# Late operand splits, the engines of the last merges, and the buffer of one output weight in a hybrid decoder layer

## The chip, the cores and the metric

The kernel runs on one core of a Trainium2 chip. The metric is the device time of one execution in microseconds (us), smaller is better. Five engines of the core work side by side, each on its own instruction stream in order: TensorE (PE, matrix products), VectorE (DVE), ScalarE (ACT), GpSimd (POOL) and SyncE (SP, which issues most loads). They wait for one another by semaphores.

## What is computed

One inference step of a one-layer decoder for a prompt of 1024 tokens and 8 samples of 4 tokens (1056 rows in all, width 1024): a sliding-window attention branch and a retention branch (4 heads, key width 128, value width 256) on one input projection, merged by sigmoid gates, projected by `w_o`, and a ConvFFN behind it. Cut to what matters here:

```python
def trunk_layer(x, pos, ...):
    xn = rms_norm(x, g_pre_mix)
    h = xn @ w_in
    q_a, k_a, v_a, q_r, k_r, v_r, gate_r, gm_a, gm_r = jnp.split(h, split_points(), axis=-1)
    ...
    o_a = banded_window_attn(q_a, k_a, v_a, pos, sinks)
    ...
    o_r, new_s = retention(qr, kr, vr, ret_s0.astype(jnp.float32))
    o_r = head_rms(o_r).reshape(B, T, V_R).astype(x.dtype)
    y_a = o_a @ w_a_proj
    y_r = (jax.nn.silu(gate_r) * o_r) @ w_r_proj
    mixed = (jax.nn.sigmoid(gm_a) * y_a + jax.nn.sigmoid(gm_r) * y_r) @ w_o
    x = x + rms_norm(mixed, g_post_mix)
    f, new_conv = conv_ffn(rms_norm(x, g_pre_ffn), conv_ctx, w_up, conv_w, conv_b, w_down)
    x = x + rms_norm(f, g_post_ffn)
```

## The kernel before

**Numbers as pairs.** Every matrix operand is held as two float32r tiles, a high part (a cast on ACT) and a low part (source minus high part, on DVE); the function `split` (and `w_split` for the input weights) does both, so a weight's split is one ACT instruction and one DVE instruction (all `L223`, with two inputs in SBUF). A product `mm3` is three matmuls: high x high, high x low, low x high (`L255` to `L257`).

**Seven products for eight.** The large projections (`w_in`, `w_r_proj`, the FFN) are computed two by two blocks by a scheme of Strassen's kind with seven products, A11, A12, A22, S1, S2, S3, S4. Its operands are sums of blocks: on the weight side, `in_split` splits seven weights for each unit of two columns; on the activation side `x_sums(j)` builds the operands `ex` of S2, S3 and A22 for each half j of the rows. A product is 12 matmuls of 128x264.

**The stream.** `stream()` is a Python generator that emits the input projection of the retention branch and of all gates, one product at each `yield`; `adv(n)` takes n products out of it. The other stages place these products between their own steps. 16 units stand in `ORDER`, each with j = 0 and 1. After some products the PSUM banks are evicted into the tile `pair` by a copy on ACT (`L926`) and additions on DVE (`L949` behind S4, `L951` behind S3). The weights' buffers are `wsp` (tags `hi` and `lo`, three buffers each) and, for each seventh split, a tile `w7x` of another pool; `NSPL` counts the splits. The raw weights (`w_raw`, loaded by SP) are freed when their last split is done.

**What stands around the stream's start.** `attn_proj(0..3)` (the attention branch's projection, which also uses `wsp`), `x_sums(0)` and `x_sums(1)`. In the last one, before the operands of S3 and A22, `first_weights` begins the first unit's splits (EARLY, five of them). Then a pool is closed and its memory goes to the pool `rs` with the constants of the rotary embedding and the samples' tiles.

**The samples.** `sample(h)` emits one head of the samples' retention step (five steps, between which `adv(3)` stands): loads, a product with the states `s0`, the state's update, and at the end `finish` (normalisation on ACT and POOL) and `turn`, two transposes on PE (`L1012`), whose result goes to `z8`.

**The prompt's retention** follows (blocks of 128 rows of each head, with `adv` in between), then the projection by `w_r_proj`: `PORD` gives its seven products; `z_weights(n)` loads and splits 14 weights (n = 0 to 13, here z0 to z13). The results go to the eight tiles `Gr[0..7]`, by evictions on ACT and DVE (`L1273` to `L1283`; `L1279` for S3 and S1, `L1283` for S4). As soon as a half of a tile is complete, `merge(m, half)` multiplies it by a gate (`L1267`, input `g_in`) and adds the other branch (`L1268`, input `a_in`): half 0 after A12 (tiles 0 to 3) and A22 (tiles 4 to 7), half 1 after S1 (tiles 4 to 7) and S4 (tiles 0 to 3). `merged_to_X` splits the merged halves into the operand of `w_o` (`xh` on ACT, `xl` on DVE). In between, `weights` loads and splits the eight parts of `w_o`, `wo[0]` to `wo[7]`; the list at its end says from which pool each takes its buffers: `wop`, `tpool` (16 buffers that are also those of the `Gr` tiles) or, for None, `wsp`.

**The output loop** runs over nine tiles of rows (`tt`), each 8 x 2 products of 128x512 in `w_part(hf, k, ...)`; the first tile runs over k in the order `LATE`. Behind it come the norm, and the first products of `w_up`, whose weights take buffers of `wsp`.

What is emitted is put in order for each engine by a scheduler of the framework, except instructions marked by `PIN` or `pinned`, which keep their place.

Of the kernel before, what the change touches and what calls it, by code (L numbers as in the profile page):

```python
# [18 lines left out]
P = 128  # L19
D = 1024  # L20
KD = D // P
# [99 lines left out]
def trunk(ctx, tc, I, O):  # L121
# [200 lines left out]
    NSPL = [0]  # L322
# [471 lines left out]
    begun = []  # L794

    def x_sums(j):

        b12 = b12_X(j)
        t2, t3, t, u1 = tiles = [p2.tile([P, 4, HW], F32, name="ts%d" % q) for q in range(4)]
        combos(j, 0, HW, tiles[:3])  # L800
        t1(j, u1, t2, V)
        split(*b12, u1)
        for p, src in ((S2, t2), (S3, t3), (A22, t)):
            if j and p == S3:
                first_weights()
                PIN[0] = True
            ex1[p, j] = [TT("ex", (P, 4, HW), F32R) for _ in range(2)]
            split(*ex1[p, j], src)
        PIN[0] = False
# [24 lines left out]
    def first_weights():  # L834

        ws = in_split(ORDER[0])
        next(ws)
        next(ws)
        begun.extend((p, next(ws)) for p in EARLY[:5])
        begun.append(ws)  # L840

# [3 lines left out]
    x_sums(1)  # L845

    ph_stack.close()
    rp = pool("rs", 1, stack=ph_stack)
# [52 lines left out]
    def stream():  # L901

        ws = begun.pop()
        ops = dict(begun)
        ops[S3] = next(ws)
# [3 lines left out]
        for i, n in enumerate(ORDER):  # L909
            for j in range(2):  # L910
# [17 lines left out]
                for p in (A11, S1, A22, S2, A12, S4, S3):  # L928
                    if p == A22:
                        if last is not None:  # L930
                            product(A22, *last)
                        if j == 0:
                            ops[A22] = next(ws)
                            ws = coming
                            if i + 1 < len(ORDER):
                                next(ws)
# [15 lines left out]
                    if p == S2:  # L952
                        flush()
                    if j and i + 1 < len(ORDER):
# [19 lines left out]
    def flush():  # L974
        while PEND:
            PEND.pop(0)()

    rcos, rsin = ST("rcos", (P, T)), ST("rsin", (P, T))
# [45 lines left out]
    def sample(h):  # L1024
# [50 lines left out]
        S.copy(out=z8[:, h], in_=turn(pt, finish(os8, NS, 1, h, 1)))  # L1075

    for n in range(2):
        load_s0(n)
    adv(18)
    for h in range(4):  # L1080
        for _ in sample(h):
            adv(3)

# [140 lines left out]
    for g in range(3):  # L1224
        load_v(g)
    coming, behind = ahead(0), None
# [13 lines left out]
    adv(len(ORDER) * 14 - 8 - 78 - 4 * NBLK - 1)  # L1240
# [19 lines left out]
    def merge(m, half):  # L1260
# [5 lines left out]
        eng = G if m < 4 else V  # L1266
# [33 lines left out]
    for pi, p in enumerate(PORD):  # L1300
# [19 lines left out]
        for m in {0: (0,), 1: (1,), 2: (2,), 3: (3, 4), 4: (5,), 5: (6,), 6: (7,)}.get(pi, ()):  # L1320
            wo.append(weights(1, D, [(lambda r: r[:, 0], w_o[m * P:(m + 1) * P, :])],
                              [wop, wop, tpool, tpool, tpool, tpool, tpool, None][m]))
# [12 lines left out]
    LATE = (0, 1, 2, 3, 4, 7, 5, 6)  # L1335
# [416 lines left out]
```

## Time and profile before

| | |
|---|---|
| three runs, median (lowest to highest) | 1674.64 us (1672.92 to 1675.68) |
| the profiled execution | 1673.6 us |
| its span, from the first to the last instruction | 1671.8 us |
| mean granted clock of TensorE | 0.997 of full speed |
| instructions | 32491 |
| HBM read, written | 184.24 MB, 87.49 MB |

The times that follow are microseconds from the start of the span. The samples' stage lies at about 300 to 412, the prompt's retention from there to about 690, the projection by `w_r_proj` and the merges up to 797, the first tile of `w_o` from 797 to 816, the FFN from about 905 to the end. A profile's row of the timeline gives the start, the duration, the engine, the line in the kernel, the operation, the tile written and the tiles read, its size, and in brackets how long the engine was idle before it and what ended that.

### The profile page before, as it was taken

To read this page: it belongs to the slowest core of one execution; us is meant where nothing else is said; L and a number is where in the kernel's file an instruction comes from. 1 tells how busy PE (TensorE), PEld (TensorE's weight loads), DVE (VectorE), ACT (ScalarE), POOL (GpSimd) and SP (SyncE) were. 2 spreads that over 40 slices of the span, in tenths; PEclk is the share of its full clock that TensorE was granted. 3 is DMA by queue.
4 is the path that set the end of the run, shared out by engine and by line. 5 is a ranking of instruction groups with operands and counts; after the bars stand their busy time and mean duration, and the time that the engine had idled before them with its cause. 6 is when DMAs were issued, how large, how long until landed. Compare 5 with 4: busy or idle time off the path is not lost.

```text
span 1671.8 us, 32491 instructions
## 1 busy us (share of the span) xinstructions
PE 1629.8 (97%) x12551; PEld 1587.6 (95%) x12551; DVE 1229.3 (74%) x2035; ACT 860.4 (51%) x1882; POOL 474.1 (28%) x686
## 2 busy tenths in 40 slices
PE   8999999898999999999999999999999999999997
PEld 7999989888999999999688999999999999999997
DVE  7887738799556566478847988888898988455476
ACT  6565634355655655554333655555555556443343
POOL 4242430456343433250412122212322223111111
PEclk9999999999999999999999999999999999999999
DMA  7312232445676775597523144545444548866664
GB/s 199 67 46 72 70 78 99 151 137 170 211 243 217 239 236 178 186 296 213 186 89 103 51 142 159 172 147 172 159 160 160 173 158 257 243 192 195 195 187 144
DMA packets 273291, 273.88 MB, mean 164 GB/s; under 512 B 23040, under 2 KB 234272, under 8 KB 273121
## 3 DMA queue, kind: packets, MB, share of 16 engines
q1 hardware_dynamic: 239377, 155.25, 32.0%
q0 software_dynamic: 33760, 116.57, 20.1%
q8 instruction: 98, 1.61, 0.4%
q14 instruction: 56, 0.46, 0.1%
HBM read 184.24 MB, written 87.49 MB: 163 GB/s over the span
## 4 chain that ended last, share of the span: by engine, by line
PE 68%; DVE 3%; DMA 2%; issue 1%; ACT 1%; SPq 0%; POOL 0%; DVEq 0%; ACTq 0%; POOLq 0%
PE ps_m L257 9%; PE ps_m L256 9%; PE ps_m L255 9%; PE ps_t L256 8%; PE ps_t L255 8%; PE ps_t L257 8%; PE ps_q L255 4%; PE ps_q L257 4%; PE ps_q L256 4%; DVE xl L223 1%; DMA zt<-in_w_r_proj 1%; PE ps_b L1155 1%; PE ps_a L1159 1%; PE ps_b L1157 1%; PE ps_t L461 0%
## 5 line engine op out<-in xcount | busy, mean ns | idle before, releaser
L255 PE MATMUL ps_q<-xh,w 128*128 128x264 f32 x512 | 152.4, 298 | 5.4 <-DVE pair L949 3.0
L223 DVE SCALAR_TENSOR_TENSOR w_lo<-w_raw,w_hi 128x1024 fp32r<-128x1024 f32 x83 | 106.7, 1290 | 65.5 <-ACT w_hi L228 59.9
L255 PE MATMUL ps_t<-xh,w_hi 128*128 128x264 f32 (+2 forms) x524 | 149.0, 284 | 0.0
L256 PE MATMUL ps_t<-xl,w_hi 128*128 128x264 f32 (+2 forms) x524 | 148.9, 284 | 0.0
L257 PE MATMUL ps_t<-xh,w_lo 128*128 128x264 f32 (+2 forms) x524 | 148.2, 283 | 0.0
L257 PE MATMUL ps_m<-xh,w_lo 128*128 128x264 f32 x512 | 145.7, 285 | 0.5 <-DVE w_lo L223 0.5
L255 PE MATMUL ps_m<-xh,w_hi 128*128 128x264 f32 x512 | 146.0, 285 | 0.0
L256 PE MATMUL ps_q<-xl,w 128*128 128x264 f32 x512 | 145.9, 285 | 0.0
L256 PE MATMUL ps_m<-xl,w_hi 128*128 128x264 f32 x512 | 145.5, 284 | 0.0
L257 PE MATMUL ps_q<-xh,w 128*128 128x264 f32 x512 | 145.4, 284 | 0.0
L223 DVE SCALAR_TENSOR_TENSOR w<-w_raw,w 128x512 fp32r<-128x512 f32 x152 | 113.3, 751 | 36.9 <-ACT w L331 35.4
L1500 DVE SCALAR_TENSOR_TENSOR c_out<-u_ext,fconst,c_out 128x1024 f32<-128x1024 f32 x96 | 122.3, 1281 | 2.0 <-ACT c_out L1496 0.5
L228 ACT CAST w_hi<-w_raw 128x1024 fp32r<-128x1024 f32 x62 | 65.2, 1052 | 104.5 <-PE ps_t L256 75.0
L331 ACT CAST w<-w_raw 128x512 fp32r<-128x512 f32 x152 | 93.9, 622 | 37.9 <-DVE w_raw L223 22.9
L255 PEld LDWEIGHTS ps_q<-xh,w 128*128 128x128 f32 x512 | 96.6, 189 | 7.5 <-DVE pair L949 4.4
L257 PEld LDWEIGHTS ps_t<-xh,w_lo 128*128 128x128 f32 x524 | 98.8, 189 | 0.0
L255 PEld LDWEIGHTS ps_t<-xh,w_hi 128*128 128x128 f32 x524 | 98.7, 188 | 0.0
L256 PEld LDWEIGHTS ps_t<-xl,w_hi 128*128 128x128 f32 x524 | 98.7, 188 | 0.0
L257 PEld LDWEIGHTS ps_m<-xh,w_lo 128*128 128x128 f32 x512 | 96.4, 188 | 0.8 <-DVE w_lo L223 0.7
L256 PEld LDWEIGHTS ps_q<-xl,w 128*128 128x128 f32 x512 | 96.6, 189 | 0.5
L256 PEld LDWEIGHTS ps_m<-xl,w_hi 128*128 128x128 f32 x512 | 96.3, 188 | 0.0
L255 PEld LDWEIGHTS ps_m<-xh,w_hi 128*128 128x128 f32 x512 | 96.3, 188 | 0.0
(447 smaller groups left out, 6045.7 us busy)
## 6 DMA issues: line engine op xcount, KB each, us to landing
w_raw<-in_w_up SPq DMA_DIRECT2D x48, 512.0 KB, 4.1
w_raw<-in_w_in SPq DMA_DIRECT2D x42, 512.0 KB, 4.6
w_raw<-s_d SPq DMA_DIRECT2D x60, 256.0 KB, 4.0
t_d<-t POOLq DMA_DIRECT2D x24, 528.0 KB, 3.9
t<-t_d POOLq DMA_DIRECT2D x24, 528.0 KB, 5.1
t<-in_w_down SPq DMA_DIRECT2D x48, 256.0 KB, 4.4
s_d<-t POOLq DMA_DIRECT2D x24, 512.0 KB, 3.5
w_raw<-in_w_down SPq DMA_DIRECT2D x36, 256.0 KB, 5.7
```

The lines of the kernel that those rows point to most:

```text
L223: pinned(V.scalar_tensor_tensor(out=out, in0=in0, scalar=1.0, in1=in1, op0=mult, op1=op))
L228: pinned(S.copy(out=hi, in_=src))
L255: TE.matmul(ps, wh, xh, start=start, stop=False, **kw)
L256: TE.matmul(ps, wh, xl, start=False, stop=False, **kw)
L257: TE.matmul(ps, wl, xh, start=False, stop=stop, **kw)
L331: S.copy(out=t[:, 0:4], in_=src)
L1155: TE.matmul(po, sT, vt, start=True, stop=tt == 0)
L1157: TE.matmul(po, q, state["s"], start=False, stop=True)
L1159: TE.matmul(pk, kt, vt, start=True, stop=True)
L1500: V.scalar_tensor_tensor(out=c[:, NS:], in0=u[:, g, NU + t:NU + t + SEQ], scalar=sc[t], in1=c[:, NS:], op0=mult, op1=add)
```

## The change

Five things change. (1) The last two operands of `x_sums(1)`, those of S3 and A22, are no longer split in `x_sums` but, by the new function `operand`, behind the first four calls of the stream; `first_weights` and `begun` go, and the pool is closed after that. (2) The splits are counted from 2 instead of 0, so the fifth split of each unit (S4), not the seventh (A22) in the first unit, takes the tile `w7x`; the stream takes the weights of S3 and A22 of the first unit later. (3) The transposes at a sample head's end are kept in a list `turns` and emitted behind the first three products after the next head's first step; the counts of `adv` follow. (4) The merges of half 1 swap engines: tiles 4 to 7 on POOL, tiles 0 to 3 on DVE; half 0 stays. (5) `wo[6]` takes its buffers from `wsp` instead of `tpool`, and the first tile of the output loop runs over k in plain order.

```diff
--- before.py
+++ after.py
@@ -319,7 +319,7 @@
         split(hi, lo, raw)
         return hi, lo
 
-    NSPL = [0]
+    NSPL = [2]
     wx = {}
 
     def w_split(src, eng):
@@ -791,7 +791,6 @@
     EARLY = (A11, S1, S2, A12, S4, S3)
     COLS = [(QR0 + P * h, KR0 + P * h) for h in range(4)]
     COLS += [(c, c + P) for b in (GR0, GA0, GM0) for c in range(b, b + D, 2 * P)]
-    begun = []
 
     def x_sums(j):
 
@@ -802,11 +801,13 @@
         split(*b12, u1)
         for p, src in ((S2, t2), (S3, t3), (A22, t)):
             if j and p == S3:
-                first_weights()
-                PIN[0] = True
-            ex1[p, j] = [TT("ex", (P, 4, HW), F32R) for _ in range(2)]
-            split(*ex1[p, j], src)
-        PIN[0] = False
+                return t3, t
+            operand(p, j, src)
+
+    def operand(p, j, src):
+
+        ex1[p, j] = [TT("ex", (P, 4, HW), F32R) for _ in range(2)]
+        split(*ex1[p, j], src)
 
     def in_split(n):
 
@@ -831,21 +832,10 @@
         yield w_split(a21, V)
         yield w_split(a22, V)
 
-    def first_weights():
-
-        ws = in_split(ORDER[0])
-        next(ws)
-        next(ws)
-        begun.extend((p, next(ws)) for p in EARLY[:5])
-        begun.append(ws)
-
     for mm in range(4):
         attn_proj(mm)
     x_sums(0)
-    x_sums(1)
-
-    ph_stack.close()
-    rp = pool("rs", 1, stack=ph_stack)
+    late = x_sums(1)
 
     def ST(name, shape, dt=F32, **kw):
         return rp.tile(list(shape), dt, name=name, **kw)
@@ -900,9 +890,10 @@
 
     def stream():
 
-        ws = begun.pop()
-        ops = dict(begun)
-        ops[S3] = next(ws)
+        ws = in_split(ORDER[0])
+        next(ws)
+        next(ws)
+        ops = {p: next(ws) for p in EARLY[:5]}
         coming = in_split(ORDER[1])
         next(coming)
         last, nh = None, 0
@@ -929,7 +920,7 @@
                     if p == A22:
                         if last is not None:
                             product(A22, *last)
-                        if j == 0:
+                        if j == 0 and i:
                             ops[A22] = next(ws)
                             ws = coming
                             if i + 1 < len(ORDER):
@@ -951,6 +942,12 @@
                         V.tensor_tensor(out=c22, in0=bk[1], in1=c22, op=add)
                     if p == S2:
                         flush()
+                    if p == S4 and S3 not in ops:
+                        ops[S3] = next(ws)
+                    if p == S3 and A22 not in ops:
+                        ops[A22] = next(ws)
+                        ws = coming
+                        next(ws)
                     if j and i + 1 < len(ORDER):
                         nxt[p] = next(ws)
                         if p == S4 and i + 2 < len(ORDER):
@@ -975,6 +972,13 @@
         while PEND:
             PEND.pop(0)()
 
+    adv(4)
+    PIN[0] = True
+    for p, t in zip((S3, A22), late):
+        operand(p, 1, t)
+    PIN[0] = False
+    ph_stack.close()
+    rp = pool("rs", 1, stack=ph_stack)
     rcos, rsin = ST("rcos", (P, T)), ST("rsin", (P, T))
     ld.dma_start(out=rcos, in_=I["rcos"])
     ld.dma_start(out=rsin, in_=I["rsin"])
@@ -1072,14 +1076,20 @@
         os8 = ST("t8", (P, 256))[:NS]
         S.copy(out=os8, in_=po[NS:2 * NS])
         V.tensor_tensor(out=os8, in0=po[0:NS], in1=os8, op=add)
-        S.copy(out=z8[:, h], in_=turn(pt, finish(os8, NS, 1, h, 1)))
-
+        o = finish(os8, NS, 1, h, 1)
+        turns.append(lambda: S.copy(out=z8[:, h], in_=turn(pt, o)))
+
+    turns = []
     for n in range(2):
         load_s0(n)
-    adv(18)
+    adv(14)
     for h in range(4):
         for _ in sample(h):
             adv(3)
+            while turns:
+                turns.pop()()
+    adv(2)
+    turns.pop()()
 
     for nm in "kv":
         pin(st.dma_start(out=O[nm + "_sample"][0].rearrange("b r k d -> b r (k d)")[:, 0:P - DS, :],
@@ -1223,6 +1233,7 @@
         load_qk(g)
     for g in range(3):
         load_v(g)
+    adv(0)
     coming, behind = ahead(0), None
     for g in range(NBLK):
         f, coming = coming, ahead(g + 1)
@@ -1237,7 +1248,7 @@
         behind = (g,) + m
     adv(1)
     tail(*behind)
-    adv(len(ORDER) * 14 - 8 - 78 - 4 * NBLK - 1)
+    adv(len(ORDER) * 14 - 8 - 80 - 4 * NBLK - 1)
     for n in range(4):
         load_z(n, quarters(ST("zt", (P, T), bufs=3)) if n < 2 else TT("z_raw", (P, 4, HW)))
     for _ in STR:
@@ -1263,7 +1274,7 @@
         for t, d in zip(ga, (gm_d[KD + m], a_d[m])):
             ld.dma_start(out=t, in_=halves_of(d)[:, :, half])
         v = halves_of(Gr[m])[:, :, half]
-        eng = G if m < 4 else V
+        eng = V if (m < 4) == half else G
         eng.tensor_tensor(out=v, in0=v, in1=ga[0], op=mult)
         eng.tensor_tensor(out=v, in0=v, in1=ga[1], op=add)
 
@@ -1319,7 +1330,7 @@
             merged_to_X(0)
         for m in {0: (0,), 1: (1,), 2: (2,), 3: (3, 4), 4: (5,), 5: (6,), 6: (7,)}.get(pi, ()):
             wo.append(weights(1, D, [(lambda r: r[:, 0], w_o[m * P:(m + 1) * P, :])],
-                              [wop, wop, tpool, tpool, tpool, tpool, tpool, None][m]))
+                              [wop, wop, tpool, tpool, tpool, tpool, None, None][m]))
     merged_to_X(1)
 
 
@@ -1332,7 +1343,7 @@
     J1B = NS + 7 * P - 3 * HW
     raws = {j: [tr.tile([P, 4, HW], F32, name="t%d" % q) for q in range(3)] for j in range(1)}
 
-    LATE = (0, 1, 2, 3, 4, 7, 5, 6)
+    LATE = range(KD)
     for tt in [0, 4, SMP, 1, 2, 3, 5, 6, 7]:
         r_ = rows(tt)
         xt = TT("xt2", (P, D))[:r_]
```

Three places show how the instructions move. The lines of the new kernel are 9 lower in the stream (`L917` was `L926`, `L934` was `L943`, `L940` was `L949`) and 11 higher from the merges on (`L1278` was `L1267`, `L1290` was `L1279`, `L1294` was `L1283`).

First, ACT at the start of the stream, before. `w7` are high parts of the first unit's weights, `y_a` results of `attn_proj`, `ex` the operands of A22 and S3 for j = 1, `pair` the first eviction:

```order
L331 CAST w7_3590<-w_raw_3539 128x512
L786 COPY y_a_3447<-ps_a_3476 128x288
L331 CAST w7_3557<-w_raw_3537 128x512
L228 CAST ex_3560<-ts1_3519 128x1056
L228 CAST ex_3564<-ts2_3520 128x1056
L926 COPY pair_3595<-ps_q2_3597 128x264
L926 COPY pair_3595<-ps_q1_3598 128x264
L926 COPY pair_3595<-ps_q0_3596 128x264
```

And in the new kernel, up to the same operands:

```order
L786 COPY y_a_3403<-ps_a_3432 128x288
L786 COPY y_a_3447<-ps_a_3448 128x384
L786 COPY y_a_3447<-ps_a_3462 128x384
L917 COPY pair_3562<-ps_q2_3564 128x264
L917 COPY pair_3562<-ps_q1_3565 128x264
L331 CAST w7_3678<-w_raw_3539 128x512
L786 COPY y_a_3447<-ps_a_3476 128x288
L331 CAST w7_3662<-w_raw_3539 128x512
L917 COPY pair_3562<-ps_q0_3563 128x264
L228 CAST ex_3619<-ts1_3519 128x1056
L228 CAST ex_3623<-ts2_3520 128x1056
```

The three evictions stood behind both operands' casts and now stand ahead of them; the fifth weight (`w7x`) has moved further up, ahead of the rows shown.

Second, DVE in the last part of `w_r_proj`, before, up to the low part of z13 (`w_lo_9772`). `Gr4` to `Gr7` are the tiles whose half 1 S1 completes, `xl` the low parts of merged halves:

```order
L1267 TENSOR_TENSOR Gr7_8834<-Gr7_8834,g_in_9568 128x2x264
L1279 TENSOR_TENSOR Gr5_8832<-ps_m_9653,Gr5_8832 128x264
L1279 TENSOR_TENSOR Gr5_8832<-ps_t_9667,Gr5_8832 128x264
L1267 TENSOR_TENSOR Gr4_8831<-Gr4_8831,g_in_9647 128x2x264
L1279 TENSOR_TENSOR Gr6_8833<-ps_m_9694,Gr6_8833 128x264
L223 SCALAR_TENSOR_TENSOR xl_110<-Gr6_8833,xh_109 128x264
L1268 TENSOR_TENSOR Gr7_8834<-Gr7_8834,a_in_9569 128x2x264
L223 SCALAR_TENSOR_TENSOR xl_110<-Gr6_8833,xh_109 128x264
L1267 TENSOR_TENSOR Gr5_8832<-Gr5_8832,g_in_9681 128x2x264
L1279 TENSOR_TENSOR Gr6_8833<-ps_t_9708,Gr6_8833 128x264
L223 SCALAR_TENSOR_TENSOR w_lo_9772<-w_raw_9768,w_hi_9771 128x1024
```

The same place in the new kernel; `w_lo_9765` is the low part of `wo[6]`:

```order
L223 SCALAR_TENSOR_TENSOR w_lo_9765<-w_raw_9762,w_hi_9764 128x1024
L223 SCALAR_TENSOR_TENSOR xl_110<-Gr6_8833,xh_109 128x264
L1290 TENSOR_TENSOR Gr6_8833<-ps_m_9694,Gr6_8833 128x264
L223 SCALAR_TENSOR_TENSOR xl_110<-Gr6_8833,xh_109 128x264
L1279 TENSOR_TENSOR Gr7_8834<-Gr7_8834,a_in_9569 128x2x264
L1290 TENSOR_TENSOR Gr6_8833<-ps_t_9708,Gr6_8833 128x264
L1290 TENSOR_TENSOR Gr7_8834<-ps_m_9728,Gr7_8834 128x264
L1290 TENSOR_TENSOR Gr7_8834<-ps_t_9742,Gr7_8834 128x264
L223 SCALAR_TENSOR_TENSOR xl_110<-Gr4_8831,xh_109 128x264
L223 SCALAR_TENSOR_TENSOR xl_110<-Gr7_8834,xh_109 128x264 x2
L1294 TENSOR_TENSOR Gr0_8827<-ps_m_9619,Gr0_8827 128x264
L223 SCALAR_TENSOR_TENSOR w_lo_9772<-w_raw_9768,w_hi_9771 128x1024
```

Ahead of z13's low part two merges of half 1 have gone, and `wo[6]`'s low part, the two evictions of `Gr7`, the `xl` of `Gr4` and `Gr7` and one eviction of `Gr0` have come.

Third, POOL's merges of half 1 in the new kernel:

```order
L1278 TENSOR_TENSOR Gr4_8831<-Gr4_8831,g_in_9647 128x2x264
L1278 TENSOR_TENSOR Gr5_8832<-Gr5_8832,g_in_9681 128x2x264
L1279 TENSOR_TENSOR Gr4_8831<-Gr4_8831,a_in_9648 128x2x264
L1279 TENSOR_TENSOR Gr5_8832<-Gr5_8832,a_in_9682 128x2x264
L1278 TENSOR_TENSOR Gr6_8833<-Gr6_8833,g_in_9722 128x2x264
L1278 TENSOR_TENSOR Gr7_8834<-Gr7_8834,g_in_9756 128x2x264
L1279 TENSOR_TENSOR Gr6_8833<-Gr6_8833,a_in_9723 128x2x264
L1279 TENSOR_TENSOR Gr7_8834<-Gr7_8834,a_in_9757 128x2x264
```

Before, the eight rows here were those of `Gr0` to `Gr3`, whose half 1 is complete only after S4.

## The prediction

> **What bounds the kernel now.** I read the page's busy shares first, then the table of TensorE's waits, then windows cut by stage, then the timelines of the stages that lose time.
>
> ```profile
> PE 1629.8 (97%) x12551; PEld 1587.6 (95%) x12551; DVE 1229.3 (74%) x2035; ACT 860.4 (51%) x1882; POOL 474.1 (28%) x686
> ```
>
> ```profile
> 283.00:330.00 47.00, 41.31 (x307) 40.23 (x307) 29.20 (x40) 18.44 (x41) 16.01 (x14) 1.00 0.46 144
> 330.00:420.00 90.00, 81.37 (x635) 77.04 (x635) 85.48 (x130) 48.26 (x132) 53.16 (x45) 1.00 0.46 148
> 420.00:690.00 270.00, 269.12 (x2079) 263.47 (x2078) 157.40 (x336) 155.27 (x380) 93.99 (x156) 1.00 0.68 214
> 690.00:777.00 87.00, 85.86 (x702) 85.33 (x701) 61.17 (x76) 47.76 (x73) 27.59 (x26) 1.00 0.83 257
> 777.00:818.00 41.00, 37.01 (x230) 33.18 (x229) 39.82 (x66) 16.59 (x38) 14.32 (x10) 0.96 0.79 234
> 818.00:1590.00 772.00, 772.00 (x6045) 754.47 (x6044) 585.27 (x907) 386.19 (x731) 168.21 (x286) 1.00 0.51 162
> ```
>
> Columns: window, its length, busy PE, PEld, DVE, ACT, POOL, then the granted clock, DMA share and GB/s. PE sets the end: its work is unchanged by the edit, so only idle or slowed PE time can come or go. The edit touches three windows with some: 5.7 us idle in 283:330, 8.6 in 330:420, 4.0 in 777:818 (with a mean clock of 0.96). In 330:420 DVE is busy 85.48 of 90, in 777:818 39.82 of 41: there DVE is the bound and PE follows it.
>
> **Stream start (283 to 330).** Three timelines of before: ACT, PE, DVE (start, length, instruction, and in brackets the idle time before it with what ended it).
>
> ```profile
> 297.19 0.62 ACT L331 CAST w<-w_raw 128x512 fp32r<-128x512 f32 x1 [1.34 <-PE ps_a L256]
> ...
> 298.53 2.04 ACT L228 CAST ex<-ts 128x1056 fp32r<-128x1056 f32 x2
> 300.48 0.94 ACT L926 COPY pair<-ps_q 128x264 f32<-128x264 f32 x3
> ```
>
> ```profile
> 300.91 0.39 PE L255 MATMUL ps_q<-xh,w 128*128 128x264 f32 x1 [2.27 <-ACT pair L926]
> ...
> 317.84 0.39 PE L255 MATMUL ps_q<-xh,w 128*128 128x264 f32 x1 [1.76 <-DVE pair L949]
> ```
>
> ```profile
> 297.85 1.51 DVE L223 SCALAR_TENSOR_TENSOR w<-w_raw,w 128x512 fp32r<-128x512 f32 x2 [10.10 <-ACT w L331]
> ...
> 305.95 0.69 DVE L223 SCALAR_TENSOR_TENSOR s<-w_raw 128x512 f32<-128x512 f32 x1 [1.87 <-DMA w_raw<-in_w_in]
> ...
> 314.03 1.46 DVE L1039 TENSOR_TENSOR v<-vs,v 32x256 fp32r<-32x256 f32 x1
> ...
> 317.36 0.43 DVE L949 TENSOR_TENSOR pair<-ps_q,pair 128x264 f32<-128x264 f32 x1
> ...
> 330.31 0.69 DVE L223 SCALAR_TENSOR_TENSOR s<-w_raw 128x512 f32<-128x512 f32 x1 [1.73 <-DMA w_raw<-in_w_in]
> ```
>
> The fifth weight split waits for `attn_proj`'s last product (ACT, 297.19), the operand casts `ex` stand ahead of the evictions, and PE waits 2.27 us. Changed: the fifth split goes to a buffer nobody holds, and the late operands stand behind the evictions. The first eviction then needs 298.53, not 300.48: about 2 us of the 2.27 go. The next unit's raw weights, freed by that split, come sooner. DVE's row from 305.95 to the second `L949` loses one weight split and `v`'s two subtractions (the second took 1.46): the 1.76 us wait goes too. The two come to about 4 us of PE. What is late next is the DVE-bound stage, which starts from the second unit's raw weights (330.31). These wait on SP behind a raw load that the fourth split of unit 1 frees; I have that some 3.3 us sooner, between 2.0 (the first wait alone) and 4.0 (both). So **A = -3.3 us**. Ends: 0, if DVE's backlog eats it, and -6, if the deferred turn's wait (next) and the smaller ones of 0.6 to 1.0 in the samples also go.
>
> **Sample turns.**
>
> ```profile
> PE ps_b L1012 <- ACT o L1006: 1.3, 1, 1.3
> ```
>
> This is a row of PE's waits (total, times, longest). One turn in four was waited for. With three products in between it is covered. Since DVE, busy 85.48 of 90, sets that stage, PE would only wait elsewhere: 0, at best the -1.3 in A's low end. Products pulled ahead are 14 + 4 for 18, and 2 at the end, so the later stages stand two products on; PE is full there (269.12 of 270): 0.
>
> **Merges and the seventh w_o weight (777 to 818).** First the loss of before, on PE, with DVE's split that ends it.
>
> ```profile
> 806.47 0.39 PE L256 MATMUL ps_m<-w_loT,xh 128*128 128x512 f32 x1
> 806.70 0.40 PE L257 MATMUL ps_m<-w_hiT,xl 128*128 128x512 f32 x1
> 807.23 0.50 PE L255 MATMUL ps_m<-w_hiT,xh 128*128 128x512 f32 x1
> 811.58 0.80 PE L256 MATMUL ps_m<-w_loT,xh 128*128 128x512 f32 x1 [3.85 <-DVE w_loT L223]
> 812.17 0.63 PE L257 MATMUL ps_m<-w_hiT,xl 128*128 128x512 f32 x1
> ...
> 815.02 0.39 PE L255 MATMUL ps_m<-w_hiT,xh 128*128 128x512 f32 x1
> ```
>
> ```profile
> 806.13 1.05 ACT L246 CAST w_hiT<-w_raw 128x1024 fp32r<-128x1024 f32 x1 [2.77 <-DVE xl L223]
> ```
>
> Full pitch of a 128x512 product is 0.23 us (806.47 to 806.70). Lost: 0.30 at 807.23, 4.12 up to 811.58, and 1.58 in the eight products from 811.58 to 815.02 (3.44 for 8 x 0.2325), where the clock is half. Together 6.0 us. The weight's buffer now comes from the weight pool, its split moves some 30 rows up DVE, and the w_o stall goes: **-6.0**. The plain order of the eight parts of the first tile costs nothing, since the seventh is no longer the late one; nor does the count of half-1 merges, eight on each engine as before.
>
> But the same rows of DVE also hold the low part of the last r_proj weight (z13), and PE was already just in time for it:
>
> ```profile
> 785.71 0.71 DVE L1267 TENSOR_TENSOR Gr<-Gr,g_in 128x528 f32<-128x528 f32 x1
> 786.33 0.43 DVE L1279 TENSOR_TENSOR Gr<-ps_m,Gr 128x264 f32<-128x264 f32 x1
> 786.67 0.43 DVE L1279 TENSOR_TENSOR Gr<-ps_t,Gr 128x264 f32<-128x264 f32 x1
> ...
> 790.23 1.22 DVE L223 SCALAR_TENSOR_TENSOR w_lo<-w_raw,w_hi 128x1024 fp32r<-128x1024 f32 x1
> ...
> 796.56 1.24 DVE L223 SCALAR_TENSOR_TENSOR xl<-Gr,xh 128x264 fp32r<-128x264 f32 x1
> 797.72 0.70 DVE L1268 TENSOR_TENSOR Gr<-Gr,a_in 128x528 f32<-128x528 f32 x1
> 798.34 2.36 DVE L223 SCALAR_TENSOR_TENSOR w_lo<-w_raw,w_hi 128x1024 fp32r<-128x1024 f32 x1
> ...
> 801.58 0.42 DVE L1283 TENSOR_TENSOR Gr<-ps_m,Gr 128x264 f32<-128x264 f32 x1
> ```
>
> ```profile
> 791.25 0.29 PE L255 MATMUL ps_m<-xh,w_hi 128*128 128x264 f32 x1
> 791.38 0.28 PE L256 MATMUL ps_m<-xl,w_hi 128*128 128x264 f32 x1
> 791.51 0.39 PE L257 MATMUL ps_m<-xh,w_lo 128*128 128x264 f32 x1
> ```
>
> ```profile
> 795.78 1.73 POOL L1267 TENSOR_TENSOR Gr<-Gr,g_in 128x528 f32<-128x528 f32 x1 [45.48 <-DVE Gr L1283]
> 797.78 1.84 POOL L1268 TENSOR_TENSOR Gr<-Gr,a_in 128x528 f32<-128x528 f32 x1 [0.27 <-DMA a_in<-a_d]
> 801.12 1.73 POOL L1267 TENSOR_TENSOR Gr<-Gr,g_in 128x528 f32<-128x528 f32 x1 [1.50 <-DVE Gr L1283]
> ```
>
> The low part is done at 791.45, and the product at 791.51 uses it. The rows from 796.56 show what a merge on POOL does to DVE: the split at 798.34 takes 2.36, not 1.22. POOL's merge starts when DVE's has ended (798.34) and holds DVE's instruction of two SBUF inputs for **1.14 us**; one such instruction slips in between two merges. Evictions, with one input in PSUM, are not held (0.42 at 801.58, under the merge of 801.12).
>
> Before, POOL's eight half-1 merges began at 795.78, behind z13. Now POOL has those of blocks 4 to 7, which are ready at 786.3. Between there and the end of z13's split DVE has, by the new order, eight instructions that can be held (two splits of 1.14, five `xl` of 0.34, a merge of 0.62: 4.6 us) and seven evictions (0.34 each, 2.4 us); these are start-to-start times, since rows overlap by some 0.09 (786.33 - 785.71 = 0.62, 786.67 - 786.33 = 0.34; `xl` has an eviction's size). Six POOL merges can get in between (6 x 1.14 = 6.8); the last two wait for a load that DVE's late merge frees. Most evictions lie under a hold; I take 0.6 us of them as open. End: 786.3 + 4.6 + 6.8 + 0.6 = 798.3, against a need at 791.3: a **new wait of 7.0 us**. ACT's cast of that weight stands behind `xh` casts that wait for the same merges, but by the same count ends some 3 us ahead of its split's turn on DVE. Bounds: nothing held, 786.3 + 4.6 + 2.4 = 793.3, a wait of 2.0; eight holds and every eviction in the open, 802.4, a wait of 11.1.
>
> A wait of 3.85 us was followed by half the clock; I charge the new one the same 1.6 us. After waits of 2.27 and 1.76 the clock was 1.00 (283:330), so at the lower bound I charge nothing. In the first w_o tile nothing more is late: its seventh weight is split near 788, the eighth about 6 us behind z13's, 10 us ahead of need. So **B = -6.0 + 7.0 + 1.6 = +2.6** (from -4.0 to +6.7).
>
> [...]
>
> **Second w_up weight.** It takes a slot that a w_o weight now holds to the end of the last w_o tile. Its split (1.2 us of DVE) stands ahead of that tile's norm. 48 products of the first w_up weight (48 x 0.12 = 5.8 us) cover it: 0; without cover, up to 2 us more.
>
> **Sum.** 1673.6 (profiled; span 1671.8 and 1.8 outside it) - 3.3 + 2.6 = **1672.9 us**. The median of the three runs shown is 1.0 above the profiled execution; the forecast is kept on the profiled one's measure and the range takes the difference in.
>
> **Rivals.**
> - *The new wait stays short.* POOL's merges start later than 786.3 or hold little, z13's split ends near 793.3, B = -4.0: 1673.6 - 3.3 - 4.0 = **1666.3**. For it: POOL's loads share SP's queue and could come late. Against: the 1.14 us hold at 798.34, and POOL idle before 795.78.
> - *The samples eat the start's gain.* DVE is busy 95% of 330:420, and POOL's 53 us there hold it too; if their overlap changes, A = 0: 1673.6 + 2.6 = **1676.2**. Against: DVE was idle 10.10 us before 297.85 and 1.73 before 330.31, so its work can start sooner.
> - *The wait at z13 is longer still: slower.* One mechanism: all eight POOL merges hold DVE ahead of that split, no eviction is hidden; wait 11.1, B = +6.7: 1673.6 - 3.3 + 6.7 = **1677.0**. The kernel gets slower than before once the wait passes 7.7 us (7.7 + 1.6 - 6.0 = 3.3). For it: 7.7 is only 0.7 from my value. Against: the last two merges' loads.
>
> **Chances and range.** Forecast (1670 to 1676) 0.55, short wait 0.25, eaten gain 0.11, longer wait 0.09. The measurement of this kernel can tell about 0.2% (3.4 us) from no change: under 1670.2 counts as faster, over 1677.0 as slower. Faster: 0.24 of the short wait and 0.07 of the forecast's low end, 0.31. Slower: half of the last two, 0.11. Same: 0.58. Low end 1664.5 (short wait with a little more from A), high end 1678 (the longest wait, or A = 0 with a wait near 8.5).
>
> **What would show it.** In the profile after: no 2.27 and 1.76 us waits near 300 and 317, and `s` of the second unit near 327; no wait for w_loT in the first w_o tile; a wait of the product line L257 or L255 for `w_lo` near 788 (791.3 - 3.3), of 7 us, with POOL's merges running side by side with long `xl` and `w_lo` on DVE, and half a clock behind it. If that wait is under 3 us, the hold is mis-sized and the time is near 1666. If the sample stage ends no sooner against 412 than before, A is wrong.

## The result and the profile after

| | before | changed |
|---|---|---|
| median (lowest to highest) of six executions each, taken in turn | 1674.43 us (1672.92 to 1675.76) | 1689.41 us (1686.39 to 1692.11) |
| ratio to before, 95% interval | | **1.0079 [1.0067, 1.0091]** |
| profiled execution; its span | 1673.6 us; 1671.8 us | 1689.39 us; 1687.5 us |
| mean granted clock | 0.997 | 0.990 |

The kernel became 15 us slower. The forecast was 1672.9 us, no change, and its range ended at 1678.0. Of all executions that follow, one, of the kernel e12, took 1765.69 us at a mean granted clock of 0.85; it is left out of that kernel's ratio.

The busy shares of the changed kernel, the first lines to compare:

```profile
PE 1634.5 (97%) x12551; PEld 1593.2 (94%) x12551; DVE 1223.9 (73%) x2035; ACT 860.7 (51%) x1882; POOL 491.3 (29%) x686
```

They tell almost nothing: as many instructions on TensorE, 4.7 us more busy time (matmuls at half clock: where the granted clock was 0.50, near 608, a 128x264 one started every 0.22 us, at 601 with a clock of 1.00 every 0.12), 97% as before. The windows tell where it went (columns as in the prediction). From the third row on they are cut at the same matmuls as those of before; the first two are not, so only their idle time can be compared (1.8 and 8.9 us of TensorE, 5.7 and 8.6 before):

```profile
281.00:328.00 47.00, 45.17 (x342) 44.53 (x340) 31.71 (x47) 21.20 (x47) 17.80 (x15) 1.00 0.45 148
328.00:415.80 87.80, 78.90 (x616) 76.41 (x616) 82.69 (x126) 46.69 (x127) 52.29 (x45) 0.98 0.48 151
415.80:699.10 283.30, 272.45 (x2078) 265.33 (x2078) 156.07 (x335) 155.49 (x381) 93.47 (x155) 0.99 0.64 204
699.10:788.90 89.80, 87.40 (x702) 86.77 (x701) 61.36 (x79) 47.74 (x75) 28.15 (x26) 0.98 0.81 252
788.90:834.20 45.30, 37.34 (x230) 34.00 (x230) 40.19 (x71) 15.59 (x36) 18.38 (x11) 0.89 0.72 221
834.20:1606.20 772.00, 772.00 (x6045) 754.24 (x6044) 583.26 (x902) 387.09 (x730) 180.35 (x285) 1.00 0.51 161
```

The third row is the surprise. It held 270.00 us before and was full; now it is 283.30 us long with 10.85 us of idle TensorE. The fifth is 45.30 instead of 41.00 us, and the FFN is unchanged at 772.00. TensorE's waits in the third window, and in the fifth (two answers; total, times, longest):

```profile
PE ps_q L255 <- DVE pair L940: 4.9, 1, 4.9
PE ps_a L1152 <- DVE state L1172: 4.8, 4, 2.0
PE ps_b L1165 <- DVE z L1188: 0.9, 1, 0.9
```

```profile
PE ps_m L257 <- DVE w_lo L223: 4.6, 1, 4.6
PE ps_m L255 <- ACT w_hi L228: 3.3, 1, 3.3
```

The second pair is the new wait at z13, which the prediction had. The first three are not in it.

**A ledger by shift.** Every kernel here issues 12551 matmuls. So for the n-th of them, its start in one profiled execution less its start in that of before is what has been lost up to there. Each row is one execution: for e4 and e12 the shortest of theirs, for e6 and e8 the longest, so their last columns lie some us below or above what the ratios say. In the table, `at 470` is the matmul that stood at 470 us before; "start" is the edit of parts 1 and 2 (late operands, the count of splits), "wo" the other home of the seventh output weight.

| kernel | ratio [95%] | 360 | 470 | 606 | 740 | 775 | 805 | 815 | 1650 |
|---|---|---|---|---|---|---|---|---|---|
| changed | 1.0079 [1.0067, 1.0091] | -4.0 | -5.1 | +8.9 | +8.9 | +11.9 | +22.2 | +16.2 | +16.2 |
| e1 start alone | 0.9992 [0.9983, 1.0002] | -3.4 | -3.4 | -4.3 | -4.0 | -2.4 | -1.6 | -1.2 | +1.2 |
| e2 turns and 80 alone | 1.0097 [1.0071, 1.0122] | -2.0 | +1.0 | +9.8 | +9.7 | +10.3 | +10.2 | +10.4 | +13.7 |
| e3 merges alone | 1.0017 [1.0006, 1.0028] | -0.3 | -0.4 | -0.3 | +0.6 | +0.9 | +7.2 | +3.1 | +5.0 |
| e4 wo alone | 0.9976 [0.9965, 0.9986] | -0.3 | -0.8 | -1.3 | -1.2 | -1.5 | +0.7 | -5.4 | -4.8 |
| e5 changed, 78 ahead | 1.0020 [1.0010, 1.0029] | -4.3 | -4.1 | -4.7 | -4.5 | -2.7 | +7.5 | +1.5 | +1.5 |
| e6 before, 80 ahead | 1.0072 [1.0055, 1.0090] | -0.2 | +1.8 | +11.6 | +12.6 | +13.9 | +14.4 | +14.3 | +16.0 |
| e7 start and wo | 0.9990 [0.9978, 1.0001] | -2.6 | -3.3 | -2.2 | -1.9 | +0.4 | +6.7 | +0.7 | +1.1 |
| e8 merges and wo | 1.0022 [1.0013, 1.0031] | +0.2 | +1.9 | +1.9 | +2.3 | +6.3 | +14.8 | +8.8 | +8.8 |
| e9 changed, quads on GpSimd | 1.0018 [1.0008, 1.0028] | -4.9 | -4.2 | -4.7 | -4.1 | -3.1 | +10.2 | +4.2 | +6.1 |
| e10 before, 76 ahead | 1.0073 [1.0058, 1.0088] | +0.2 | +4.6 | +7.4 | +13.5 | +13.1 | +13.9 | +13.9 | +14.2 |
| e11 before, 82 ahead | 1.0024 [1.0014, 1.0033] | -0.2 | -0.4 | +0.4 | +4.0 | +3.3 | +3.1 | +3.9 | +5.2 |
| e12 e9 without merges | 0.9970 [0.9958, 0.9982] | -4.2 | -4.8 | -5.4 | -5.6 | -5.6 | -2.6 | -8.6 | -8.4 |

The changed kernel's row reads: the start gains 4 to 5 us, the attention stage loses 14.0 (from -5.1 to +8.9; half of it by 560, half at 607), the stretch from 740 to 775 loses 3, z13 loses 10.3, the first output tile gains 6.0.

**The loss at 607.** TensorE waited 4.93 us, and its granted clock was half (0.50 in 605:610) from 604.1 on for 6.8 us. What it waited for is an eviction on VectorE; the rows of VectorE, then of TensorE:

```profile
598.19 0.41 DVE L1172 SCALAR_TENSOR_TENSOR state<-state,ps_a 128x256 f32<-128x256 f32 x1
605.87 0.89 DVE L223 SCALAR_TENSOR_TENSOR zt<-zt 128x256 f32<-128x256 f32 x2 [7.26 <-DMA zt<-in_w_r_proj]
606.67 0.43 DVE L940 TENSOR_TENSOR pair<-ps_q,pair 128x264 f32<-128x264 f32 x1
```

```profile
601.93 0.28 PE L257 MATMUL ps_q<-xh,w 128*128 128x264 f32 x1
607.15 0.59 PE L255 MATMUL ps_q<-xh,w 128*128 128x264 f32 x1 [4.93 <-DVE pair L940]
```

VectorE has nothing to do for 7.26 us. At the head of its line stand sums of a quad of `w_r_proj` whose load has not landed (a quad is four blocks of that weight, loaded together into a `zt` tile; `quad_sums` adds and subtracts them on VectorE and stores the result to `r_d`); the eviction behind them takes 0.43 us and could have run long before. So VectorE, which the profile names as the releaser, only passes the delay on. The load comes from SyncE (`L289` is `quad_load`); SyncE's line in the changed kernel, then GpSimd's store of the quad before:

```profile
566.61 0.36 SPq L1126 DMA_DIRECT2D qk<-qk_d  x1
567.40 0.37 SPq L819 DMA_DIRECT2D w_raw<-in_w_in  x1
581.55 0.36 SPq L1126 DMA_DIRECT2D qk<-qk_d  x1
582.00 0.97 SPq L289 DMA_DIRECT2D zt<-in_w_r_proj  x2
...
599.12 2.40 SPq L289 DMA_DIRECT2D zt<-in_w_r_proj  x2
```

```profile
592.06 0.80 POOL L300 DMA_DIRECT2D r_d<-zt  x1 [7.16 <-DVE zt L223]
```

SyncE issues nothing from 567.77 to 581.55: a `qk` load at the head of its line waits for TensorE to release its buffer. The quad load behind it goes out at 582.00 (568.65 before), so its sums and their store to `r_d` are late (592.06), and the next quad's load waits for that store to land: it is issued at 599.12 (585.67 before), and has landed when VectorE starts again. Before, VectorE's line has the same order at this place, the sums ahead of the eviction, but the load is in time:

```profile
592.08 1.81 DVE L223 SCALAR_TENSOR_TENSOR zt<-zt 128x256 f32<-128x256 f32 x4 [3.48 <-DMA zt<-in_w_r_proj]
...
597.63 0.43 DVE L949 TENSOR_TENSOR pair<-ps_q,pair 128x264 f32<-128x264 f32 x1
```

So two things make the wait: a late load, and sums that stand ahead of the eviction in VectorE's line. The late load comes from SyncE's line. Its waits between 420 and 640, before and changed:

```profile
SPq L1116 <- PE ps_b L1157: 72.8, 19, 13.4
...
SPq L289 <- DMA r_d<-zt: 0.8, 1, 0.8
```

```profile
SPq L1126 <- PE ps_b L1167: 70.4, 16, 13.7
...
SPq L289 <- DMA r_d<-zt: 9.6, 2, 6.6
```

A long wait of `qk` was there before too (13.4, longest). New is that a quad load stands behind it, and then one behind the other's store.

**The loss ahead of it.** The other 7.0 us, from 470 to 560, come with five waits of 0.72 to 2.02 us, four of them behind `state`. Just ahead of the longest, VectorE was idle 3.81 us for a raw weight of the stream, not for a quad. What made these waits is not followed here.

### The profile page after: what moved, and what is told of

It is laid out like the page before. It is cut to its first block, busy times and chain, and to the rows that moved or that the text cites. A ratio compares the mean times of both kernels' runs of the same rounds, so it can differ in the third digit from the quotient of the medians.

```text
span 1687.5 us, 32488 instructions
## 1 busy us (share of the span) xinstructions
PE 1634.5 (97%) x12551; PEld 1593.2 (94%) x12551; DVE 1223.9 (73%) x2035; ACT 860.7 (51%) x1882; POOL 491.3 (29%) x686
## 4 chain that ended last, share of the span: by engine, by line
PE 65%; DMA 5%; DVE 4%; issue 2%; ACT 1%; POOL 1%; SPq 0%; DVEq 0%; POOLq 0%; ACTq 0%
PE ps_m L257 9%; PE ps_m L255 9%; PE ps_m L256 9%; PE ps_t L256 7%; PE ps_t L255 7%; PE ps_t L257 7%; PE ps_q L255 4%; PE ps_q L257 4%; PE ps_q L256 4%; DMA zt<-in_w_r_proj 2%; DMA w_raw<-r_d 1%; DMA r_d<-zt 1%; PE ps_b L1165 1%; DVE xl L223 1%; PE ps_a L1169 1%
## 5 line engine op out<-in xcount | busy, mean ns | idle before, releaser
L223 DVE SCALAR_TENSOR_TENSOR w<-w_raw,w 128x512 fp32r<-128x512 f32 x152 | 107.8, 709 | 36.7 <-ACT w L331 36.0
L255 PE MATMUL ps_q<-xh,w 128*128 128x264 f32 x384 | 114.7, 299 | 7.0 <-DVE pair L940 6.8
L255 PE MATMUL ps_q<-ex,w 128*128 128x264 f32 x384 | 114.3, 298 | 6.9 <-DVE pair L942 6.8
L256 PE MATMUL ps_q<-ex,w 128*128 128x264 f32 x384 | 110.0, 287 | 0.0
L257 PE MATMUL ps_q<-xh,w 128*128 128x264 f32 x384 | 109.9, 287 | 0.0
L257 PE MATMUL ps_q<-ex,w 128*128 128x264 f32 x384 | 109.8, 286 | 0.0
L256 PE MATMUL ps_q<-xl,w 128*128 128x264 f32 x384 | 109.7, 286 | 0.0
L255 PE MATMUL ps_m<-xh,w 128*128 128x264 f32 x352 | 100.0, 284 | 0.0
L256 PE MATMUL ps_m<-xl,w 128*128 128x264 f32 x352 | 100.0, 284 | 0.0
L257 PE MATMUL ps_m<-xh,w 128*128 128x264 f32 x352 | 99.9, 284 | 0.0
```

Source lines behind the costliest of these rows:

```text
L223: pinned(V.scalar_tensor_tensor(out=out, in0=in0, scalar=1.0, in1=in1, op0=mult, op1=op))
L255: TE.matmul(ps, wh, xh, start=start, stop=False, **kw)
L256: TE.matmul(ps, wh, xl, start=False, stop=False, **kw)
L257: TE.matmul(ps, wl, xh, start=False, stop=stop, **kw)
```

## The experiments

Each ran in three rounds beside the kernel before on the same chip (the twelfth in five). The cuts of code leave out lines at `...`. The first four take the change apart. For the loss in the attention stage two theories stood at first: C, the count of products ahead of that stage (80 for 78), and R, the other rotation of the weights' buffers (splits counted from 2).

**e1: parts 1 and 2.** The edits of the change up to the stream's loop, with `adv(14)`, immediate turns and 78 products ahead.

> The kernel before with the late operands and the count of splits alone (parts 1 and 2); turns, merges and wo[6] as before, 78 products ahead of the retention. Theory C (the count: the retention stage loses its 13 us because it stands two products further on in the stream): about -4 us, ratio 0.9975, no wait over 1 us between 420 and 690. Theory R (the rotation: the seventh-split buffer now holds S4's weight, raw loads come free later, and DVE waits for them in the retention stage): -4 + 13 = about +9 us, ratio 1.005, with waits for state and pair of 1 to 5 us between 470 and 610.

No measurable change in the whole. The first 690 us gain 4 us, as A had it; they are given back from 740 on, a little at a time. The attention stage loses nothing, so R falls: the rotation is here, the count is not.

**e2: part 3, the turns, with 80 products ahead.**

```diff
-        S.copy(out=z8[:, h], in_=turn(pt, finish(os8, NS, 1, h, 1)))
...
+        o = finish(os8, NS, 1, h, 1)
+        turns.append(lambda: S.copy(out=z8[:, h], in_=turn(pt, o)))
...
+            while turns:
+                turns.pop()()
+    adv(2)
+    turns.pop()()
...
-    adv(len(ORDER) * 14 - 8 - 78 - 4 * NBLK - 1)
+    adv(len(ORDER) * 14 - 8 - 80 - 4 * NBLK - 1)
```

> The kernel before with the deferred turns and the two more products alone (part 3, count 80). Theory C: about +12 us (13 less the 1.3 us wait at L1012), ratio 1.007, with the long waits between 470 and 610. Theory R: 0 to -1.3 us, ratio 0.999 to 1.000, and the retention stage as full as before.

The loss in the attention stage is here (8.8 us from 470 to 606), with the same wait near 608.

**e3: part 4, the merges. e4: part 5, the weight.**

```diff
-        eng = G if m < 4 else V
+        eng = V if (m < 4) == half else G
```

```diff
-                              [wop, wop, tpool, tpool, tpool, tpool, tpool, None][m]))
+                              [wop, wop, tpool, tpool, tpool, tpool, None, None][m]))
...
-    LATE = (0, 1, 2, 3, 4, 7, 5, 6)
+    LATE = range(KD)
```

> The kernel before with the swapped merges of half 1 alone (part 4). Theory P (POOL's merges hold DVE's instructions of two SBUF inputs ahead of z13's split): waits of 6 to 8 us at z13's products with half the clock behind them, +8 to +10 us less what the wo[6] stall of 6 us shrinks by, so +3 to +10, ratio 1.002 to 1.006. Rival W (wo[6]'s split, which now stands ahead of z13's, and not POOL, makes z13 late): no wait over 1 us at z13, 0 to -4 us.

> The kernel before with wo[6] in the weight pool and the plain order of k alone (part 5). Theory P: the w_o stall (6.0 us with its half clock) goes, z13 is late by the extra split at most (1.1 us): -4 to -6 us, ratio 0.9964 to 0.9976. Rival W: z13 late by 5 us or more, -1 us to +3 us.

The weight alone gains 0.24%, as theory P had it. The merges alone lose 0.17%, but neither kernel has the changed kernel's 8 us of waits at z13 (1.2 us in e3, 1.0 in e4): e3 fits neither of its two theories.

**e5 and e6: is it the count or the deferral?** e5 is the changed kernel with 78 ahead; e6 is the kernel before with 80.

```diff
-    adv(2)
     turns.pop()()
...
-    adv(len(ORDER) * 14 - 8 - 80 - 4 * NBLK - 1)
+    adv(len(ORDER) * 14 - 8 - 78 - 4 * NBLK - 1)
```

> The whole change, but without the two products that it puts between the last turn and the attention stage: the last turn stands right behind the fourth head's sample, and 78 products go ahead of that stage as before, not 80; the turns of the other heads stay deferred. Theory C (the loss of 13 us in the attention stage comes from the count: with 80 ahead, each quad's products, loads and evictions meet the matrix stream at another place): the stage is as full as before, no wait near 605, and the sum is start -4, merges +10.3 with its clock, w_o -6.0: 0 to +3 us, ratio 1.000 to 1.002. Rival D (deferring the turns itself costs it, by VectorE and ScalarE work that comes later): the 13 us stay, ratio near 1.008.

> The kernel before, with nothing changed but that two more products go ahead of the attention stage (80 instead of 78) and two fewer behind it. Theory C (the count): a wait of 3 to 5 us near 390 or 607 with a half clock behind it, +10 to +13 us at the end of the stage, ratio 1.006 to 1.008. Rival D (deferral): no change, ratio 1.000.

e5 has no loss in the stage (-4.1 at 470, -4.7 at 606), and e6, whose edit moves two products and nothing else, has nearly all of it: 11.8 us from 360 to 606, against 12.9 in the changed kernel. SyncE's waits of e6 between 420 and 640, and VectorE's row at the wait:

```profile
SPq L1117 <- PE ps_b L1158: 75.1, 17, 13.7
...
SPq L289 <- DMA r_d<-zt: 6.9, 1, 6.9
```

```profile
608.29 0.89 DVE L223 SCALAR_TENSOR_TENSOR zt<-zt 128x256 f32<-128x256 f32 x2 [7.43 <-DMA zt<-in_w_r_proj]
```

The same rows as in the changed kernel. It is the count; deferring the turns costs nothing that can be seen in e5. (e2 has a wait of 3.5 us near 390 and goes from -2.0 at 360 to +1.7 at 420, which neither e5 nor the changed kernel does.)

**e9: is it SyncE's line?**

```diff
-    def quad_load(w, m, pt, kk, q):
+    def quad_load(w, m, pt, kk, q, eng=None):
...
-            pin(ld.dma_start(out=q[:, :, u * P:u * P + P],
+            pin((eng or ld).dma_start(out=q[:, :, u * P:u * P + P],
...
-            quad_load(w_r, h, 0, tt // 3, quads[h])
+            quad_load(w_r, h, 0, tt // 3, quads[h], st)
```

> The changed kernel, with the two loads that fetch a quad of w_r_proj in the attention stage issued by GpSimd instead of SyncE; all else as changed, 80 products ahead. Theory Q (the wait at 607 comes from SyncE's line: a quad's load stands behind a qk load that waits 13.7 us for TensorE, so the quad's sums and their store are late and the next tile of that ring is late): the wait of 4.9 us at 607 and its half clock go, +1.9 us instead of +8.9 at 606, about -7 us at the end, ratio about 1.0037; the +6 between 470 and 560 stays. Rival: the wait is one of the tile ring whoever issues the load (the quad's buffer itself is late, behind the gate's multiplication on VectorE): the 607 wait stays, ratio 1.008. A third way: the loads now wait on GpSimd's queue for their buffer and hold back the stores behind them, and the wait moves to another place: 1.008 or more.

More went than was expected: not only the 7 us at 607 but also the 7 ahead of it. With 80 products ahead the stage now loses nothing (-4.2, -4.7), and VectorE's waits for these tiles between 420 and 640 fall from 21.6 us (five waits) to 6.3 (three). But this does not show that SyncE's line was the cause. The edit asks for one thing, and the framework's scheduler answers with more: from 455 on the instructions of VectorE, ScalarE and TensorE also stand in another order than in the changed kernel. GpSimd's rows of the two loads that SyncE had issued at 582.00 and 599.12, then VectorE's rows of the eviction and of the second quad's sums:

```profile
578.23 1.55 POOL L289 DMA_DIRECT2D zt<-in_w_r_proj  x2
...
601.27 1.55 POOL L289 DMA_DIRECT2D zt<-in_w_r_proj  x2
```

```profile
592.20 0.43 DVE L940 TENSOR_TENSOR pair<-ps_q,pair 128x264 f32<-128x264 f32 x1 [0.21 <-issue]
...
605.89 0.42 DVE L223 SCALAR_TENSOR_TENSOR zt<-zt 128x256 f32<-128x256 f32 x1 [0.57 <-DMA zt<-in_w_r_proj]
```

The products run 6.6 us ahead of the changed kernel's here (-4.7 for +1.9 at 590), so against them both loads are issued later than SyncE issued them, by 2.8 and 8.8 us. The wait is gone because the eviction now stands ahead of the sums.

All the kernels together show that both conditions are needed. The load is the later of these two, its time less the kernel's shift at 590; the loss is the shift at 606 less that at 597:

| kernels | load issued at | sums and eviction on VectorE | loss at 607 |
|---|---|---|---|
| before, e1, e3, e4, e5, e7, e8 | 585.1 to 586.2 | sums first | at most 0.1 |
| changed, e2, e6 | 597.2 to 597.7 | sums first | 5.9 to 7.4 |
| e9 to e12 | 596.7 to 606.3 | eviction first | at most 0.6 |

**e10 and e11: other counts** (76: `adv(16)` ahead of the samples; 82: `adv(4)` behind them).

> The kernel before with 76 products ahead of the attention stage instead of 78; the samples begin two products earlier, and two more products stand behind the stage. If more products ahead are worse in themselves (the stage's work comes later against the products): no loss, 1673 to 1675 us, ratio 0.999 to 1.000. If it is a matter of how the two orders fall against each other, a loss of 3 to 13 us may stand here too, with the SyncE row of a quad load that waits for the store of the one before as its sign. No theory forecasts a gain of over 3 us, since the stage has 0.9 us of waits before.

> The kernel before with 82 products ahead of the attention stage. If more ahead is worse in itself: at least the +13.9 us that 80 gave, ratio 1.008 or more. If it is a matter of how the two orders fall against each other: anything from 0 to +13, and where the loss is under 4 us, SyncE's row of a quad load that waits for the store of the one before should be missing.

Fewer is as bad as two more, and four more costs little: the loss does not grow with the count. My sign for it holds only in part: e11 has a quad load that waits 5.7 us for a store and loses nothing before 606, and the table says why: its eviction stands ahead of the sums. e10 loses its 13 us in small waits from 392 on, which I did not follow. What is settled is the wait at 607 with 80 products; for 76 the cause is open.

**e7 and e8: do the parts add?** The edits of e1 and e4 together, and of e3 and e4.

> The late operands at the stream's start and the other home for one weight, without deferred turns, extra products or merges on VectorE. If the two gains add as each measured alone: -1.3 - 4.0 = -5.3 us, ratio 0.9968. If the start's -4 us, which were given back behind 750 in the run of that part alone, are kept: -8 to -9 us, ratio 0.995. If the start's shift brings the half clock near 758 again, it is the former.

> The kernel before with the merges of the second half on VectorE's side swapped and the other home for one weight, nothing else. If the two only add as each measured alone: +2.8 - 4.0 = -1.2 us, ratio 0.9993. If together they make the wait at the last weight of r_proj that the changed kernel shows (GpSimd's merges and the seventh tile's split both stand on VectorE ahead of it): waits of 8 us there and the half clock, +10.3 - 6.0 = +4.3 us, ratio 1.0026.

e8 decides between its two theories: 0.9993 would be the sum, 1.0022 [1.0013, 1.0031] was measured. TensorE's waits from 775 on, in e3, then e8:

```profile
PE ps_m L255 <- DVE Gr L1283: 2.5, 1, 2.5
PE ps_m L256 <- DVE w_loT L223: 1.6, 1, 1.6
PE ps_m L257 <- DVE w_lo L223: 1.2, 1, 1.2
...
```

```profile
PE ps_m L257 <- DVE w_lo L223: 4.5, 1, 4.5
PE ps_m L255 <- ACT w_hi L228: 1.2, 1, 1.2
```

Alone, the merges cost z13 1.2 us of waits; with `wo[6]`'s split also ahead of it, 5.7. e7 met neither of its two cases: 0.9990 [0.9978, 1.0001] is above both 0.9968 and 0.995, so these two gains do not add. Near 758, where the expectation has half the clock again, that of e1 was 1.00 (736 to 776). e7 has no long wait; its gain goes in short ones at 767, 793 and 796 (1.43 us at 793, 1.75 at 796): its shift goes from +0.4 at 775 to +6.7 at 805, some 3 us more than these last two waits come to; what makes the rest is not shown.

**e12: e9 without the merges** (`eng = G if m < 4 else V`), the best that the runs suggested.

> The changed kernel with the quads' loads on GpSimd, and the merges on the engines of before; late operands, deferred turns, 80 products ahead and the other home for the weight stay. If the losses are the two that the runs named (the quad loads in the attention stage, the merges together with the seventh tile's split at the last weight of r_proj), the stage is full, the start's -4 us stand until 750, the wait at the last weight is at most the 2 us that the run without merges showed (with some half clock up to 8), and w_o's stall of 6.0 is gone: -4 + 0 to 8 - 6.0 - 0 = -10 to -2 us, ratio 0.994 to 0.999. Rival (the wait at the last weight belongs to the seventh tile's split alone, whatever the merges): waits of 8 us there as with the merges, +4 us, ratio 1.002.

The rival falls: `wo[6]` is split early here too, and z13's waits are these (e12, from 775 on):

```profile
PE ps_m L257 <- DVE w_lo L223: 1.2, 1, 1.2
PE ps_t L255 <- DVE Gr L1290: 1.0, 2, 0.5
```

So the merges' place costs some 8 us where that split is early, measured twice: e9 less e12, (1.0018 - 0.9970) x 1675 = 8.0, and e8 less e4, (1.0022 - 0.9976) x 1675 = 7.7. A third pair gives less: e5 less e7, which differ by the merges and the deferral, (1.0020 - 0.9990) x 1675 = 5.0, since e7 has the short waits and the loss of 6.3 us just told. e12 beats both kernels: 0.9970 [0.9958, 0.9982]. Its executions ran from 1665.2 to 1673.5 us. e4, two small edits, gives 0.9976, which the intervals do not tell apart from e12.

## Why the prediction was wrong, step by step

**The failed step: "the later stages stand two products on; PE is full there (269.12 of 270): 0".** That stage lost 14.0 us in the changed kernel, nearly all of the result. A full TensorE says that nothing was late before; it says nothing of how near the others were to being late. Half of the loss is followed to its source: the two products moved a quad load behind a `qk` load that waits over 13 us on SyncE, that made the next quad's load late too, and the eviction that TensorE needs stands behind the sums of that next quad. I looked at engines' order, not at SyncE's, though the moved `adv` stands between its loads. e6 shows the count's price by itself, 1.0072, and e5 that without it the kernel would have come out at 1.0020. That the load has to be late and the sums ahead of the eviction, the table over all kernels shows; that SyncE's line makes the load late is read from the rows of the changed kernel and of e6, and no run isolates it. What makes the 7 us ahead of 560 stays open.

**A, the stream's start: right.** Forecast -3.3; at 360 the changed kernel stands at -4.0, e1 at -3.4, e12 at -4.2. The rival "the samples eat the start's gain" did not happen there. In e1 the gain was used up by the end (+1.2), behind 740, so A was a gain at its place and no gain in time by itself.

**The turns: right at their place.** No cost is seen from the deferral in e5.

**The output weight: right.** Forecast -6.0; from 805 to 815 the changed kernel goes from +22.2 to +16.2, that is -6.0.

**The wait at z13: the right mechanism, 1.7 us too small.** GpSimd's merges, and what VectorE does under them, up to z13's split:

```profile
797.33 4.00 POOL L1278 TENSOR_TENSOR Gr<-Gr,g_in 128x528 f32<-128x528 f32 x2 [36.53 <-DVE Gr L1290]
801.28 2.96 POOL L1279 TENSOR_TENSOR Gr<-Gr,a_in 128x528 f32<-128x528 f32 x2
805.23 2.76 POOL L1278 TENSOR_TENSOR Gr<-Gr,g_in 128x528 f32<-128x528 f32 x2 [0.99 <-DVE Gr L1290]
807.94 2.94 POOL L1279 TENSOR_TENSOR Gr<-Gr,a_in 128x528 f32<-128x528 f32 x2
```

```profile
798.47 1.67 DVE L223 SCALAR_TENSOR_TENSOR w_lo<-w_raw,w_hi 128x1024 fp32r<-128x1024 f32 x1
...
803.01 1.80 DVE L1279 TENSOR_TENSOR Gr<-Gr,a_in 128x528 f32<-128x528 f32 x1
804.73 0.42 DVE L1290 TENSOR_TENSOR Gr<-ps_t,Gr 128x264 f32<-128x264 f32 x1
...
805.75 3.97 DVE L223 SCALAR_TENSOR_TENSOR xl<-Gr,xh 128x264 fp32r<-128x264 f32 x3
809.64 0.42 DVE L1294 TENSOR_TENSOR Gr<-ps_m,Gr 128x264 f32<-128x264 f32 x1
809.99 1.98 DVE L223 SCALAR_TENSOR_TENSOR w_lo<-w_raw,w_hi 128x1024 fp32r<-128x1024 f32 x1
```

Three `xl` take 3.97 us where one takes 0.44 alone, a merge 1.80 for 0.71. From 798.47 to the split's end at 811.97 the eight instructions with two SBUF inputs took 7.1 us longer, start to start, than unheld; the forecast was six holds, 6.8. But the evictions did not lie under the holds: five stood in the open, 1.7 us against the 0.6 that I allowed. Less the shift of 11.9 that the kernel had there, the split ended at 800.0, not 798.3, and TensorE needed it at 791.3, as forecast: 8.7 us late, and half the clock behind it (0.50 in 812:815) for 1.6, as charged; 10.3 in all against 8.6. The wait thus passed the 7.7 us that the rival "the wait is longer still" had as its turning point: without the loss in the attention stage the kernel would have been slightly slower by that rival, not by the forecast, as e5 and e9 are (1.0020 and 1.0018).

**Not foreseen: +3 us between 740 and 775.** Two short waits for one weight of `w_r_proj`, 1.04 and 0.75 us, and half the clock (0.50) for 3.4 us behind them (below), less a wait of 0.53 us for the next weight, 96 matmuls further on, which was there before and is not in the changed kernel. In the other kernels the waits for these two weights lie between 0 (e4, e11) and 2.0 us (e8), with and without each part. Why they grow here stays open.

Sum: at 470 -5.1, then +14.0, +3.0, +10.3 and -6.0 give the +16.2 of the last column; the spans differ by 15.7.

## What to carry to other kernels

When a change alters how many steps stand ahead of an interleaved stage, compare the order on the queues that issue loads, above all the load that waits longest for a buffer and what stands behind it: a full engine in the window is no proof of slack. Where the engine that is waited for was itself idle, follow its own wait; here TensorE, VectorE, a tile ring, a store, and at last SyncE's line. Where a scheduler sets the order, compare the orders of all engines between two runs before the edit's text is taken for the only difference: e9 removed the wait by another way than its edit was written for. And two edits that are each harmless to one deadline (the merges' holds, an early split) need their sum worked out on that deadline.

## What the runs showed of the hardware that was not expected

The clock can fall behind two short waits. In the changed kernel, TensorE waited 1.04 and 0.75 us for one weight; in e5, 1.10 and 0.75 for the next one, 96 matmuls further on. The windows of the changed kernel, then of e5 (the eighth number is the granted clock):

```profile
764.00:767.00 3.00, 1.21 (x8) 0.80 (x8) 1.65 (x3) 1.88 (x4) 0.00 (x0) 1.00 0.87 233
767.00:768.00 1.00, 1.00 (x11) 1.00 (x10) 1.00 (x4) 0.84 (x1) 0.00 (x0) 0.98 0.45 102
768.00:771.00 3.00, 3.00 (x16) 3.00 (x15) 1.93 (x4) 1.05 (x1) 0.00 (x0) 0.50 0.63 233
```

```profile
763.00:766.00 3.00, 1.32 (x8) 1.11 (x9) 2.09 (x4) 2.02 (x3) 0.00 (x0) 1.00 0.59 175
766.00:770.00 4.00, 4.00 (x35) 4.00 (x34) 4.00 (x6) 2.90 (x3) 0.00 (x0) 1.00 0.44 140
```

TensorE was busy 1.21 of 3 us in the one and 1.32 in the other; the first paid half the clock from 768 to 771 (0.50), at a time when it was full again, the second paid nothing (1.00 from 766 to 770). e8 waited 1.25 and 0.76 us at the changed kernel's products and paid too (a clock of 0.50 from 762 to 764). So near-equal waits brought half the clock in two of these three executions and none in the third. Where it came it lasted 3.4 us in the changed kernel, which costs some 1.7 us (an estimate: half of 3.4); a forecast can give such waits a chance of that, not a price. What decides between the two is not shown by any run here.
